# A state recurrence over 96 chunks: 95 steps in sequence, or an up-sweep and a down-sweep with steps of 1, 2, 4, 8 and 16 chunks; and twelve weight splits moved from GpSimd to VectorE

## The chip, the cores and the metric

The kernel runs on one core of a Trainium2 chip. It is one program, one launch. The metric is the device time of that launch in microseconds. Of the core's engines five appear below: TensorE (PE in the profile; PEld is its weight load), VectorE (DVE), ScalarE (ACT), GpSimd (POOL) and SyncE (SP), which here only starts transfers.

## The reference

The kernel computes one layer over 512 latent tokens (8 rows of a grid 64 wide) with 256 context tokens, model width 1024, all in float32. Cut to what matters here:

```python
hx = modulate(x, ...); hc = modulate(ctx, ...)            # RMSNorm, scale, shift
u_x, k_x, v_x, q_x, ga_x, gb_x = split(hx @ w_in)         # 512, 512, 512, 512, 1024, 1024
u_c, k_c, v_c = split(hc @ w_in[:, :1536])
# S5: per direction (forward, backward), 32 groups, 64 complex states each
s_ctx = scan(lam, B u_c)                 # s[t] = lam * s[t-1] + B u[t] over the 256 context tokens
s_lat = scan(lam, B u_x, s0=s_ctx end)   # goes on over the 512 latent tokens
y     = d * u_x + sum over directions of Re(C s_lat)      # only the latent y is wanted
branch_a = glu(gelu(y)) @ w_branch_a
branch_b = neighbourhood_attention(q_x, k_x, v_x, k_c, v_c, bias) @ w_branch_b   # 8 heads of 64
x = x + gate1 * ((sigmoid(ga_x) * branch_a + sigmoid(gb_x) * branch_b) @ w_out)
x = x + gate2 * peer(modulate(x, ...))   # product-key retrieval of 128 experts for each token
```

The recurrence is linear, so any grouping of its steps that multiplies by the right powers of lam gives the same states. Of the context only the state at its end is used.

## The kernel before, in words

**Chunks.** The kernel cuts the 768 tokens into 96 chunks of 8 (`TC = 8`): 32 of the context (`CC`), then 64 latent ones (`CL`). TensorE computes for each chunk what its own tokens add to the state at its end, into the tile `E` of shape [128, 2, 32, 97]: 128 partitions (64 states forward, 64 backward, the latter stored in reversed order), real and imaginary part, 32 groups, and 97 chunk positions, position 0 being zero. The chunk is the innermost index: neighbouring chunks are 4 bytes apart, neighbouring groups 388. Over the chunks the recurrence is E[p] += lam^8 * E[p-1]. The tile `L8` ([128, 2, 2, 32]) holds lam^8 for the complex product: `L8[:, 0]` its real part twice, `L8[:, 1]` its imaginary part with both signs.

**The scan.** `scan_step` (L588 to L595) is one step of it: four VectorE instructions TENSOR_TENSOR on 128x64 elements (two products, their sum, the addition into E[p]). L597 calls it for p = 1 to 95. The states at the 64 latent chunks' starts are copied into the tile `S`, forward ones by GpSimd (L618), backward ones in reversed order by ScalarE (L619), two copies of 64x2048 each. `S` is read by `y_part` (L646), which computes eight parts of y on TensorE. The states' pool (with `E`) is closed behind the q projections (L630), and what `y_load` (L636) fetches for `y_part` takes its place.

**Projections and their weights.** `project` (L447 is the last of the lines of its matmuls) multiplies a 1024x128 block of weights with the activations in three passes: the weights are split into a high part `whi` (a cast on ScalarE, L174) and the rest `wlo` (a subtraction, L175, 128x1024), and TensorE does whi*high, whi*low, wlo*high. `w_ahead` has the loads and the splits of the next blocks issued ahead; `whi` and `wlo` have two buffers each. Blocks 0 to 3 are u, 4 to 7 k, 8 to 11 v, 12 to 15 q; then come the blocks of the merge, the first of them for gate b. `PJE = lambda m: m>3` (L57) names the engine of the subtraction that `project(m)` has done ahead: GpSimd from k on (of two engines `(dve, gp)[PJE(m)]`), VectorE before.

**Attention and what lies beside it.** From L736 on 32 items (4 row pairs by 8 heads) go through three stages: `att_a` scores on TensorE (L685, L686), adds a bias (VectorE, L687), takes a maximum (L689) and an exponential (ScalarE, L691); `att_b` transposes the probabilities (L698) and copies them (L700); `att_c` multiplies by v (L716). Beside them TensorE does gate b's projections, the eight `y_part`s, and then glu, both branches, gates and merge, in an order that a string gives (`MERGE`). At 356 us, while the merge goes on, the second modulation begins: GpSimd multiplies 32 blocks of its weights (`wm`, L791) as they arrive. The PEER part takes the rest, from about 545 us on.

**Order.** The instructions of one engine run in the order of its queue. That order isn't the program's: the layer that records the kernel interleaves independent work by an estimate of its own, which the listings of the next section but one show. Rows from L1048 and L1049 used below are the last folds of one-hot products in PEER: bf16, rows of 16 elements (32 bytes); L1048 at 128x256 reads two neighbouring elements of each row, L1049 one.

Of the kernel before, what the change touches and what calls it, by code (L numbers as in the profile page):

```python
# [10 lines left out]
F32 = mybir.dt.float32  # L11
# [6 lines left out]
ALU = mybir.AluOpType  # L18
# [10 lines left out]
G = 32  # L29
HG = 16  # L30
TC = 8
CL = SEQ // TC
CC = CTXL // TC
NCK = CL + CC
# [19 lines left out]
WQE = lambda p, i: p or i%2  # L54
CHE = lambda t, n: 0
GE = lambda c: c%4==3
PJE = lambda m: m>3  # L57
LDO = "spxxxxccwwwwwwww1wwww1wwww1r"
CEARLY = 0
FC0 = 6  # L60
# [26 lines left out]
def tile_hybrid(ctx, tc, A, out, dbg=None):  # L87
    nc = tc.nc
    sy, act, dve, gp, pe = nc.sync, nc.scalar, nc.vector, nc.gpsimd, nc.tensor

    def open_pool(**kw):
        cm = tc.tile_pool(reuse_waits="tile", **kw)
        return cm, cm.__enter__()

    def close_pool(*cms):
        for cm in cms:
            cm.__exit__(None, None, None)
# [13 lines left out]
    def bank(tag="mm", bufs=None):  # L111
        bufs = bufs or nb[tag]
        return (psA if tag in ("kk", "yy") else ps).tile([128, 512], F32, tag=tag, name=tag, bufs=bufs)
# [11 lines left out]
    L8 = const.tile([128, 2, 2, G], F32, name="L8")  # L125
# [67 lines left out]
    def w_next(want, eng=gp):  # L193
        i = wpos[2]
        assert wseq[i][:2] == want, (wseq[i], want)
        w_ahead(i + 1, i + 1, eng)
        wpos[2] += 1
        w_ahead(i + 3, i + 2, eng)
        return wsp.pop(i)
# [138 lines left out]
    n = 1  # L338
# [114 lines left out]
    def project(m, ctx_too, eng=None):  # L453
        eng = eng or (dve, gp)[PJE(m)]
        w = w_next(("win", m), eng)
        a = bank()
        mm3(a, w, hxh, hxl, KD)
        if not ctx_too:
            return a, None
        c = bank("mc", 1)  # L460
        mm3(c[:, :CTXL], w, hch, hcl, KD)
        return a, c[:, :CTXL]
# [23 lines left out]
    ecm, ep = open_pool(name="ep", bufs=1, side="right")  # L486
    E = ep.tile([128, 2, G, NCK + 1], F32, name="E")
# [88 lines left out]
    for o in SEQ1:  # L576
        m = nxt[o]
# [7 lines left out]

    kcm, kp_ = open_pool(name="kp", bufs=1)

    def scan_step(p_):  # L588
        ta = ep.tile([128, 2, G], F32, name="ta", tag="ta", bufs=2)
        tb_ = ep.tile([128, 2, G], F32, name="tb_", tag="tb_", bufs=2)  # L590
        pr = E[:, :, :, p_ - 1]
        dve.tensor_tensor(ta, pr, L8[:, 0], op=ALU.mult)  # L592
        dve.tensor_tensor(tb_, pr[:, ::-1], L8[:, 1], op=ALU.mult)
        dve.tensor_tensor(ta, ta, tb_, op=ALU.add)  # L594
        dve.tensor_tensor(E[:, :, :, p_], E[:, :, :, p_], ta, op=ALU.add)  # L595

    for p_ in range(1, NCK):  # L597
        scan_step(p_)

    for m in range(4):  # L600
        k_proj(m)
# [4 lines left out]
    for m in range(4):  # L606
# [4 lines left out]
        for j0, n in ((0, 4), (4, 3)):  # L611
            p = bank("tp")
# [10 lines left out]
    for m in range(4):  # L623
        a, _ = project(12 + m, False)
        av = a.rearrange("p (r j c) -> p r j c", r=8, c=16)
        for e in range(2):
            s, z = slice(64 * e, 64 * e + 64), slice(64 * (1 - e), 64 * (1 - e) + 64)
            gp.memset(qT[2 * m + e][z], 0.0)
            act.activation(qT[2 * m + e][s].rearrange("p (j r c) -> p r j c", r=8, c=16), av[s], AF.Copy, scale=0.125)
    close_pool(ecm)  # L630

    ycm, yp = open_pool(name="yp", bufs=1, side="right")
    Y = yp.tile([128, TC, SSMW // 2], F32, name="Y")
# [132 lines left out]
    for i in range(4):  # L766
        p = bank("tp")
        uL = uLs[i]
        yr = slice(64 * (i // 2), 64 * (i // 2) + 64)
        for n_ in range(TC):  # L770
            pe.transpose(p[:, n_ * CL:(n_ + 1) * CL], Y[yr, n_, i % 2 * 128:i % 2 * 128 + 128], ident[yr, yr])
        dve.scalar_tensor_tensor(uL, uL, dsk[:, i:i + 1], p.rearrange("p (n c) -> p n c", c=CL),
                                 op0=ALU.mult, op1=ALU.add)
# [70 lines left out]
    for o in MERGE:  # L844
        m = cnt[o]
# [106 lines left out]
    for half in range(2):  # L952
        p = bank("tp")
# [426 lines left out]
```

## Time and profile before

| | |
|---|---|
| median of three runs | 1874.2 us (1873.22 to 1884.75) |
| the profiled execution | 1876.31 us, span 1874.5 us |
| mean TensorE clock in it | 0.963 of full speed |
| busy: PE, DVE, ACT, POOL | 1727.8, 1499.0, 808.0, 659.0 us |
| scan on DVE | 95 steps, from 134.0 to 284.9 us |
| k, v and q projections on PE | 140.5 to 226 us |

How to read it: the profile tells for every instruction when it started, how long it took and, where its engine had been idle, which instruction released it. The span is the time from the first to the last instruction. An engine's idle time costs only where the end of the program waits for it, and the page's chain of waits lists the work of which that holds. The clock is a share of TensorE's full speed: 0.5 is 1.2 GHz, 1.0 is 2.4 GHz. Shapes are partitions x elements.

### The profile page before, as it was taken

What the parts mean: (1) busy time and instruction counts of PE and PEld (TensorE: products, weight loads), DVE (VectorE), ACT (ScalarE), POOL (GpSimd) and SP (SyncE); (2) the same over time, 40 slices, a digit from 0 to 9 for tenths busy, and PEclk for the clock granted to TensorE, in tenths of its full rate; (3) what the DMA queues carried; (4) which work ended last, traced back from release to release, by engine and by line L of the source; (5) the groups of instructions that cost most, each with busy time, mean ns of one, the idle gap of its engine ahead of it and who ended that gap; (6) DMA issues with size and microseconds to landing.
All of it is one profiled execution on the core that took longest, in us unless ns stands there. A gap on an engine that the chain in (4) does not pass through costs nothing.

```text
span 1874.5 us, 27846 instructions
## 1 busy us (share of the span) xinstructions
PE 1727.8 (92%) x9941; PEld 1505.1 (80%) x9941; DVE 1499.0 (80%) x3111; ACT 808.0 (43%) x1276; POOL 659.0 (35%) x500
## 2 busy tenths in 40 slices
PE   4989879989999989997479999999999999999997
PEld 1778657767779989986369899999999999998885
DVE  7899995587669998999879788788888888884445
ACT  5362245455555435666433333333333333333333
POOL 3553201166523730010233445444445544440002
PEclk8999989999999999998589999999999999999998
DMA  7342114576744435757599899999999999994432
GB/s 278 114 135 83 62 54 112 175 262 210 254 147 148 143 110 159 216 172 212 146 383 361 293 331 329 341 353 350 321 344 357 319 338 347 327 346 144 127 113 79
DMA packets 186331, 426.18 MB, mean 227 GB/s; under 512 B 25552, under 2 KB 91216, under 8 KB 186192
## 3 DMA queue, kind: packets, MB, share of 16 engines
q1 hardware_dynamic: 84816, 231.44, 36.5%
q0 software_dynamic: 36864, 134.23, 20.0%
q10 hardware_dynamic: 64512, 58.73, 9.7%
q8 instruction: 78, 1.28, 0.3%
q14 instruction: 61, 0.50, 0.1%
HBM read 388.72 MB, written 35.62 MB: 226 GB/s over the span
## 4 chain that ended last, share of the span: by engine, by line
PE 71%; DVE 18%; DMA 4%; issue 3%; ACT 2%; POOL 2%; ACTq 0%; SPq 0%; DVEq 0%; POOLq 0%
PE acc L1251 9%; PE acc L1252 9%; PE acc L1253 9%; PE yy L447 5%; PE yy L445 5%; PE yy L446 5%; PE kk L447 5%; PE kk L445 5%; PE kk L446 5%; PE mm L447 2%; PE mm L446 2%; PE mm L445 2%; DVE E L595 2%; DVE ta L592 1%; DVE ta L594 1%
## 5 line engine op out<-in xcount | busy, mean ns | idle before, releaser
L174 ACT CAST whi<-wraw 128x1024 fp32r<-128x1024 f32 (+1 forms) x212 | 213.6, 1008 | 165.5 <-issue 49.9
L175 DVE TENSOR_TENSOR wlo<-wraw,whi 128x1024 fp32r<-128x1024 f32 (+1 forms) x174 | 225.1, 1294 | 56.9 <-ACT whi L174 49.4
L1134 POOL DMA_INDIRECT gu<-in_pu_dram,idx x128 | 173.8, 1357 | 262.5 <-DVE gj L1141 217.4
L1134 POOL DMA_INDIRECT gu<-in_pv_dram,idx x128 | 167.0, 1305 | 161.1 <-DVE gacc L1152 135.4
L1233 DVE TENSOR_TENSOR wlo<-wraw,whi 128x1024 fp32r<-128x1024 f32 x128 | 157.5, 1231 | 41.4 <-ACT whi L1232 37.6
L1152 DVE SCALAR_TENSOR_TENSOR gacc<-gu,av,gacc 128x1024 f32<-128x1024 f32 x127 | 162.6, 1281 | 25.5 <-DMA gu<-in_pv_dram,idx 25.0
L447 PE MATMUL yy<-hth,wlo 128*128 128x384 f32 x512 | 174.9, 342 | 3.6 <-DVE wlo L175 3.6
L1141 DVE SCALAR_TENSOR_TENSOR gj<-gu,hrow 128x1024 bf16<-128x1024 f32 x128 | 156.0, 1219 | 23.4 <-DMA gu<-in_pu_dram,idx 22.9
L445 PE MATMUL kk<-hth,whi 128*128 128x384 f32 x512 | 173.3, 338 | 1.0 <-ACT ring L932 1.0
L445 PE MATMUL yy<-hth,whi 128*128 128x384 f32 x512 | 173.9, 340 | 0.0
L446 PE MATMUL yy<-htl,whi 128*128 128x384 f32 x512 | 173.9, 340 | 0.0
L447 PE MATMUL kk<-hth,wlo 128*128 128x384 f32 x512 | 172.9, 338 | 0.6 <-DVE wlo L175 0.5
L446 PE MATMUL kk<-htl,whi 128*128 128x384 f32 x512 | 172.7, 337 | 0.0
L1232 ACT CAST whi<-wraw 128x1024 fp32r<-128x1024 f32 x128 | 134.0, 1047 | 81.5 <-PE yy L446 30.8
L175 POOL TENSOR_TENSOR wlo<-wraw,whi 128x1024 fp32r<-128x1024 f32 x38 | 96.1, 2532 | 91.5 <-ACT whi L174 87.8
L1120 ACT ACTIVATE gs<-mm 128x512 f32<-128x512 f32 x96 | 95.1, 1088 | 61.4 <-PE mm L1118 59.6
L791 POOL TENSOR_TENSOR wm<-wm,cb 128x1024 f32<-128x1024 f32 x32 | 82.4, 2575 | 87.8 <-DMA wm<-in_wmodT_dram 43.2
L447 PE MATMUL mm<-hxh,wlo 128*128 128x512 f32 x256 | 102.2, 399 | 6.6 <-DVE wlo L175 6.6
L445 PE MATMUL mm<-hxh,whi 128*128 128x512 f32 x256 | 100.0, 395 | 2.6 <-ACT whi L174 2.6
L447 PEld LDWEIGHTS yy<-hth,wlo 128*128 128x128 f32 x512 | 97.2, 190 | 5.7 <-DVE wlo L175 4.2
L446 PE MATMUL mm<-hxl,whi 128*128 128x512 f32 x256 | 100.8, 394 | 0.0
L445 PEld LDWEIGHTS kk<-hth,whi 128*128 128x128 f32 x512 | 96.4, 188 | 3.6 <-ACT ring L932 1.6
(2079 smaller groups left out, 4636.7 us busy)
## 6 DMA issues: line engine op xcount, KB each, us to landing
wraw<-in_puT_dram SPq DMA_DIRECT2D x128, 512.0 KB
wraw<-in_pv_dram SPq DMA_DIRECT2D x128, 512.0 KB
Gt_d<-gs ACTq DMA_DIRECT2D x24, 1024.0 KB
gch<-Gt_d ACTq DMA_DIRECT2D x32, 768.0 KB
wraw<-in_win_dram SPq DMA_DIRECT2D x32, 512.0 KB
wm<-in_wmodT_dram SPq DMA_DIRECT2D x32, 512.0 KB
wraw<-in_wq_dram SPq DMA_DIRECT2D x32, 512.0 KB
wm<-in_wm_dram SPq DMA_DIRECT2D x16, 512.0 KB
```

Of the source, the lines that this page charges most:

```text
L174: act.copy(hi[:, :kn], raw[:, :kn])
L175: i = eng.tensor_sub(lo[:, :kn], raw[:, :kn], hi[:, :kn].bitcast(F32))
L445: pe.matmul(o, hi[:, k], xh, start=(k == 0), stop=False)
L446: pe.matmul(o, hi[:, k], xl, start=False, stop=False)
L447: pe.matmul(o, lo[:, k], xh, start=False, stop=(k == kn - 1))
L1134: gp.indirect_dma_start(out=u, out_offset=None, in_=A[tab], in_offset=bass.IndirectOffsetOnAxis(ap=ix[:, s:s + 1], axis=0))
L1141: dve.scalar_tensor_tensor(jk, u, 1.0, hrow, op0=ALU.mult, op1=ALU.mult, accum_out=av[:, s:s + 1])
L1152: dve.scalar_tensor_tensor(gacc, u, av[:, s:s + 1], gacc, op0=ALU.mult, op1=ALU.add)
L1233: dve.tensor_sub(lo, w, hi.bitcast(F32))
L1251: pe.matmul(acc[t][half], wh_[:, ts], hi[:, cs], start=(j == 0), stop=False)
L1252: pe.matmul(acc[t][half], wh_[:, ts], lo[:, cs], start=False, stop=False)
L1253: return pe.matmul(acc[t][half], wl_[:, ts], hi[:, cs], start=False, stop=(j == 127))
```

## The change

The scan's 95 steps are replaced by 16 calls of `carry(l, first, step, n)`. One call does n chunk positions at once: the positions first, first + step, ... get lam^(8*2^l) times the value 2^l positions before. It is four VectorE instructions on 128x64xn elements. The powers lam^16 to lam^128 are computed by 24 small instructions (four times six, up to 128x32 or 128x64 elements).

- Context, up-sweep only: l = 0 to 4 with n = 16, 8, 4, 2, 1. It leaves the right value in position 32, the end of the context.
- Handover to the first latent chunk: l = 0, n = 1.
- Latent chunks, up-sweep l = 0 to 4 with n = 31, 15, 7, 3, 1, then down-sweep l = 4 to 0 with n = 1, 3, 7, 15, 31.

The innermost index of these instructions is the position, in steps of 2 << l elements: 8 bytes at l = 0, 16 to 128 bytes at l = 1 to 4 (n = 1 has no neighbours but the groups, 388 bytes apart). At l = 0 there are 16 + 1 + 31 + 31 = 79 positions, at l = 1 to 4 there are 15 + 26 + 26 = 67. Both products read `E`, both additions read and write it. A new pool holds the powers and the products' tiles, until the states' pool is closed.

The second part is `PJE = lambda m: 0`: the twelve subtractions (L175) that were on GpSimd in the k, v and q projections, for blocks 5 to 15 and the first block of the merge, are on VectorE.

```diff
-PJE = lambda m: m>3
+PJE = lambda m: 0
...
-    def scan_step(p_):
-        ta = ep.tile([128, 2, G], F32, name="ta", tag="ta", bufs=2)
-        tb_ = ep.tile([128, 2, G], F32, name="tb_", tag="tb_", bufs=2)
-        pr = E[:, :, :, p_ - 1]
-        dve.tensor_tensor(ta, pr, L8[:, 0], op=ALU.mult)
-        dve.tensor_tensor(tb_, pr[:, ::-1], L8[:, 1], op=ALU.mult)
-        dve.tensor_tensor(ta, ta, tb_, op=ALU.add)
-        dve.tensor_tensor(E[:, :, :, p_], E[:, :, :, p_], ta, op=ALU.add)
-
-    for p_ in range(1, NCK):
-        scan_step(p_)
+    sccm, scp = open_pool(name="scp", bufs=1, side="right")
+    lam = [L8]
+    for l in range(4):
+        a_, b_ = lam[-1], scp.tile([128, 2, 2, G], F32, name=f"lam{l}")
...
+        lam.append(b_)
+
+    def carry(l, first, step, n):
+
+        ta = scp.tile([128, 2, G, 31], F32, name="ta", tag="ta", bufs=1)[:, :, :, 0:n]
+        tb_ = scp.tile([128, 2, G, 31], F32, name="tb_", tag="tb_", bufs=1)[:, :, :, 0:n]
+        d = 1 << l
+        to = E[:, :, :, first:first + (n - 1) * step + 1:step]
+        fr = E[:, :, :, first - d:first - d + (n - 1) * step + 1:step]
+
+        def bc(j):
+            return lam[l][:, j].rearrange("p r (g o) -> p r g o", o=1).to_broadcast([128, 2, G, n])
+
+        dve.tensor_tensor(ta, fr, bc(0), op=ALU.mult)
+        dve.tensor_tensor(tb_, fr[:, ::-1], bc(1), op=ALU.mult)
+        dve.tensor_tensor(to, to, ta, op=ALU.add)
+        dve.tensor_tensor(to, to, tb_, op=ALU.add)
+
+    for l in range(5):
+        carry(l, 2 << l, 2 << l, CC >> (l + 1))
+    carry(0, CC + 1, 1, 1)
+    for l in range(5):
+        carry(l, CC + (2 << l), 2 << l, (CL >> (l + 1)) - 1)
+    for l in (4, 3, 2, 1, 0):
+        carry(l, CC + (3 << l), 2 << l, (CL >> (l + 1)) - 1)
...
-    close_pool(ecm)
+    close_pool(sccm, ecm)
```

Lines behind the scan are 25 later in the changed kernel (L687 is L712 there, L619 is L644). How the two kernels' instructions stand in the queues:

VectorE before, at the place where attention begins. L592 to L595 are a scan step (tiles `ta`, `tb_`, `E`), L687 is the attention's first bias addition and L689 its maximum:

```order
L592 TENSOR_TENSOR ta<-E,L_78 128x64
L593 TENSOR_TENSOR tb__2042<-E,L_78 128x64
L687 TENSOR_TENSOR mm<-mm,bs 128x256
L594 TENSOR_TENSOR ta<-ta,tb__2042 128x64
L689 TENSOR_REDUCE nm<-mm 128x1
L595 TENSOR_TENSOR E<-E,ta 128x64
L592 TENSOR_TENSOR ta<-E,L_78 128x64
```

Seventy-seven of the 95 steps stand ahead of that addition in the queue, and the rest of them are interleaved with the attention's own instructions.

VectorE now, at the same place. L612 to L615 are the four instructions of a carry (here the last two of the down-sweep, l = 1 and l = 0; the elements are 64 times the positions, and 1984 is 64x31), L175 the splits, L712 the attention's first addition:

```order
L612 TENSOR_TENSOR ta<-E,lam_1582 128x64x15
L613 TENSOR_TENSOR tb__1699<-E,lam_1582 128x64x15
L614 TENSOR_TENSOR E<-E,ta 128x64x15
L615 TENSOR_TENSOR E<-E,tb__1699 128x64x15
L612 TENSOR_TENSOR ta<-E,L_78 128x1984
L613 TENSOR_TENSOR tb__1705<-E,L_78 128x1984
L175 TENSOR_TENSOR wlo<-wraw,whi 128x1024
L614 TENSOR_TENSOR E<-E,ta 128x64x31
L175 TENSOR_TENSOR wlo<-wraw,whi 128x1024
L615 TENSOR_TENSOR E<-E,tb__1705 128x64x31
L175 TENSOR_TENSOR wlo<-wraw,whi 128x1024 x2
L712 TENSOR_TENSOR mm<-mm,bs 128x256
```

The whole scan and all the splits of the projections stand ahead of the attention's first addition now.

ScalarE before, around its copies of the states (`S<-E`). L672 starts the load of a bias, L691 is the exponential, L700 copies transposed probabilities:

```order
L700 COPY PT<-tp 128x256
L691 ACTIVATE P,ssum<-mm,nm 128x512
L672 DMA bs<-in_bias_dram 128x256
L700 COPY PT<-tp 128x256
L691 ACTIVATE P,ssum<-mm,nm 128x512
L619 COPY S<-E 64x2048 x2
L672 DMA bs<-in_bias_dram 128x256 x2
L700 COPY PT<-tp 128x256
L691 ACTIVATE P,ssum<-mm,nm 128x512
```

ScalarE now. L174 is the cast of a weight split, L640 a copy of v, L654 the two copies out of a q projection, L697 the start of a bias load:

```order
L640 COPY V_1962<-tp 128x4x128
L174 CAST whi<-wraw 128x1024
L640 COPY V_1963<-tp 128x3x128
L654 ACTIVATE q_2264<-mm 64x8x4x16 x2
L644 COPY S<-E 64x2048 x2
L697 DMA bs<-in_bias_dram 128x256 x2
L654 ACTIVATE q_2264<-mm 64x8x4x16 x2
L174 CAST whi<-wraw 128x1024
L697 DMA bs<-in_bias_dram 128x256 x2
L174 CAST whi<-wraw 128x1024
L654 ACTIVATE q_2265<-mm 64x8x4x16 x2
```

The copies of the states stood among the attention's items; they stand now inside the q projections, ahead of q block 1's copies and of the casts for q block 3 and for the merge's first block.

## Rows read from the trace of the kernel before

**Rows 1.** The page's part 1: busy time (share of the span) and instructions of each engine.

```profile
PE 1727.8 (92%) x9941; PEld 1505.1 (80%) x9941; DVE 1499.0 (80%) x3111; ACT 808.0 (43%) x1276; POOL 659.0 (35%) x500
```

**Rows 2.** The page's part 4, the chain of waits: shares of the span by engine.

```profile
PE 71%; DVE 18%; DMA 4%; issue 3%; ACT 2%; POOL 2%; ACTq 0%; SPq 0%; DVEq 0%; POOLq 0%
```

**Rows 3.** Windows: start:end, length, then busy time of each engine, TensorE clock, DMA share, GB/s.

```profile
140.50:226.00 85.50, 85.46 (x471) 73.73 (x468) 79.42 (x234) 26.58 (x60) 31.59 (x35) 1.00 0.25 79
226.00:236.00 10.00, 0.00 (x0) 0.00 (x0) 8.99 (x39) 0.00 (x0) 0.00 (x0) 0.71 0.00 0
236.00:246.00 10.00, 0.08 (x1) 0.08 (x2) 9.14 (x38) 2.20 (x4) 0.00 (x0) 0.50 0.04 13
246.00:251.26 5.26, 4.90 (x14) 3.46 (x14) 5.08 (x19) 2.60 (x6) 0.00 (x0) 0.56 0.22 74
251.26:262.00 10.74, 10.74 (x77) 7.97 (x78) 10.08 (x34) 6.27 (x17) 0.21 (x1) 1.00 0.26 76
...
356.35:545.00 188.65, 172.57 (x724) 135.22 (x725) 138.56 (x133) 104.03 (x171) 104.89 (x47) 0.98 0.67 225
```

**Rows 4.** Timeline of PE: start, duration, line, instruction [idle before it, and its releaser].

```profile
245.92 1.12 PE L698 MATMUL tp<-ident,P 128*128 128x128 f32 x4 [19.96 <-ACT P L691]
```

**Rows 5.** Timeline of DVE: three scan steps, and the attention's first add.

```profile
214.48 2.27 DVE L594 TENSOR_TENSOR ta<-ta,tb__1904 128x64 f32<-128x64 f32 x1
217.10 0.27 DVE L592 TENSOR_TENSOR ta<-E,L 128x64 f32<-128x64 f32 x1
...
217.59 0.23 DVE L594 TENSOR_TENSOR ta<-ta,tb__1910 128x64 f32<-128x64 f32 x1
...
218.16 0.27 DVE L592 TENSOR_TENSOR ta<-E,L 128x64 f32<-128x64 f32 x1
...
242.51 0.42 DVE L687 TENSOR_TENSOR mm<-mm,bs 128x256 f32<-128x256 f32 x1
```

**Rows 6.** Timeline of POOL: one split of projection weights.

```profile
214.28 2.39 POOL L175 TENSOR_TENSOR wlo<-wraw,whi 128x1024 fp32r<-128x1024 f32 x1 [3.31 <-ACT whi L174]
```

**Rows 7.** One line's instructions: duration min/median/max in ns, first and last start.

```profile
L595 DVE TENSOR_TENSOR E<-E,ta x95: 223/278/2512, 134.0 to 284.9; 128x64 f32<-128x64 f32 x95
```

**Rows 8.** Timeline of DVE: other TENSOR_TENSORs, contiguous.

```profile
15.70 0.21 DVE L330 TENSOR_TENSOR tg<-pw 128x64 f32<-128x64 f32 x1
...
17.93 0.28 DVE L331 TENSOR_TENSOR pw<-pw 128x128 f32<-128x128 f32 x1
...
108.57 0.41 DVE L334 TENSOR_TENSOR Gc<-PG,crt 128x256 f32<-128x256 f32 x1
...
678.76 1.19 DVE L175 TENSOR_TENSOR wlo<-wraw,whi 128x1024 fp32r<-128x1024 f32 x1
```

**Rows 9.** Groups of DVE instructions by shape: busy us, mean ns of one, idle before.

```profile
L1048 DVE TENSOR_TENSOR oh<-oh 128x256 bf16<-128x256 bf16 x8 | 3.2, 428 | 0.0
...
L1049 DVE TENSOR_TENSOR v<-oh 128x128 f32<-128x128 bf16 x2 | 0.7, 375 | 0.0
```

**Rows 10.** Timeline of ACT: casts of projection weights, each at a projection's end.

```profile
157.63 1.05 ACT L174 CAST whi<-wraw 128x1024 fp32r<-128x1024 f32 x1 [2.32 <-PE mc L446]
...
201.44 1.05 ACT L174 CAST whi<-wraw 128x1024 fp32r<-128x1024 f32 x1 [1.90 <-PE mc L446]
...
207.45 1.05 ACT L174 CAST whi<-wraw 128x1024 fp32r<-128x1024 f32 x1 [4.20 <-issue]
...
218.59 1.05 ACT L174 CAST whi<-wraw 128x1024 fp32r<-128x1024 f32 x1 [3.17 <-issue]
...
219.67 1.20 ACT L629 ACTIVATE q<-mm 64x512 f32<-64x512 f32 x2
```

**Rows 11.** One line's instructions: ACT's copies of the states.

```profile
L619 ACT COPY S<-E x2: 1901/1904/1908, 287.1 to 288.9; 64x2048 f32<-64x2048 f32 x2
```

**Rows 12.** Waits: engine (SPq is SP's queue), line, releaser: total us, times, longest.

```profile
POOL wm L791 <- DMA wm<-in_wmodT_dram: 43.2, 24, 3.5
...
SPq L643 <- DMA bs<-in_bias_dram: 13.8, 5, 4.1
```

More of the change, by code (lines that the diff above doesn't have):

```diff
@@ L586, in tile_hybrid @@
     kcm, kp_ = open_pool(name="kp", bufs=1)
-    def scan_step(p_):
-        ta = ep.tile([128, 2, G], F32, name="ta", tag="ta", bufs=2)
-        tb_ = ep.tile([128, 2, G], F32, name="tb_", tag="tb_", bufs=2)
-        pr = E[:, :, :, p_ - 1]
-        dve.tensor_tensor(ta, pr, L8[:, 0], op=ALU.mult)
-        dve.tensor_tensor(tb_, pr[:, ::-1], L8[:, 1], op=ALU.mult)
-        dve.tensor_tensor(ta, ta, tb_, op=ALU.add)
-        dve.tensor_tensor(E[:, :, :, p_], E[:, :, :, p_], ta, op=ALU.add)
-    for p_ in range(1, NCK):
-        scan_step(p_)
+    sccm, scp = open_pool(name="scp", bufs=1, side="right")
+    lam = [L8]
+    for l in range(4):
+        a_, b_ = lam[-1], scp.tile([128, 2, 2, G], F32, name=f"lam{l}")
+        ta = scp.tile([128, G], F32, tag="lt", name="lt", bufs=2)
+        dve.tensor_mul(ta, a_[:, 1, 1], a_[:, 1, 1])
+        dve.tensor_mul(b_[:, 0, 0], a_[:, 0, 0], a_[:, 0, 0])
+        dve.tensor_sub(b_[:, 0, 0], b_[:, 0, 0], ta)
+        dve.scalar_tensor_tensor(b_[:, 1, 1], a_[:, 0, 0], 2.0, a_[:, 1, 1], op0=ALU.mult, op1=ALU.mult)
+        dve.tensor_copy(b_[:, 0, 1], b_[:, 0, 0])
+        dve.tensor_scalar(b_[:, 1, 0], b_[:, 1, 1], -1.0, None, op0=ALU.mult)
+        lam.append(b_)
[18 more added lines that the diff above has]
+        carry(l, CC + (3 << l), 2 << l, (CL >> (l + 1)) - 1)
     for m in range(4):
```

## The prediction

> **What bounds the kernel now.** I read the page first: TensorE is busy 92% of the span [rows 1], and 71% of the chain of waits is its own, 18% VectorE's [rows 2]. The reader is to see there that a change to VectorE's work is worth something only where TensorE stands still. So the next view is the windows. TensorE is without a gap through the k, v and q projections (85.46 of 85.50 us), then does nothing in two windows of 10 us while VectorE is 90% busy, works at half clock (0.50 to 0.56) until 251.26, and is full again from there [rows 3]. The timelines name the cause: TensorE's pause of 19.96 us ends at 245.92 with an exponential of the attention [rows 4], and the addition ahead of that exponential ran on VectorE only at 242.51 [rows 5]. It stood in VectorE's queue behind 77 steps of the scan, which lasts from 134.0 to 284.9 [rows 7].
>
> One step takes 1.06 us (217.10 to 218.16). While GpSimd does a split (2.39 us, [rows 6]), the step's instruction takes 2.27 us in place of 0.23 [rows 5]; that happens 11 times between 139 and 222 us. So the scan costs 95 x 1.06 = 101 us and about 11 x 2.05 = 23 us of stalls. The price of the present order is what lies between 225.96, where the q projections end (245.92 less 19.96), and 251.26: 25.3 us, in which TensorE did 4.90 us of half-clock work, 2.45 us at full clock.
>
> **The change: what the new scan costs.** VectorE's price in two kinds of access has to be found.
>
> - Contiguous: 64, 128 and 256 elements took 0.21, 0.28 and 0.41 us [rows 8]. The slope is (0.41 - 0.21)/192 = 1.04 ns an element. Started back to back they lie about 0.07 us further apart than their elements; one that needs the result of the one just before takes some 0.12 us more (the steps' own pitch of 1.06 us for four shows it).
> - One element, then a jump: `ta<-E` at 64 elements, each 388 bytes from the next, took 0.27 us where 0.21 is the contiguous price [rows 5, 8]: +0.9 ns an element. L1049 at 128 elements 32 bytes apart took 0.375 for 0.28 [rows 9, 8]: +0.75. I take the middle, 1.04 + 0.83 = 1.87 ns an element.
> - Two neighbours, then a jump: L1048 at 256 took 0.428 for 0.41 [rows 9, 8], so nothing.
>
> The carries at l = 0 have 78 positions with neighbours 8 bytes apart, 78 x 64 x 4 = 19,968 elements; those at l of 1 and more (16 to 128 bytes apart) and the handover have 68, 17,408 elements. No row shows steps of 8 bytes. I take the contiguous price, since two elements lie in 16 bytes there as two lie in 32 in L1048. Sum: 19,968 x 1.04 = 20.8, 17,408 x 1.87 = 32.6, 64 x 0.07 = 4.5, 32 x 0.12 = 3.8: **61 us**. If all went at 1.04 it would be 47, if all at 1.87 it would be 78. The 24 small instructions add about 3 us.
>
> The Trainium skill, SBUF — State Buffer (Specifications), speaks against the upper levels: lines of 16 bytes, full bandwidth only with at least two accesses to a line. The rows agree for single elements, 0.375 for 0.28 us. By the two accesses every level from l = 1 on pays and level 0 goes free, the 61 us that the rows give by themselves. The page also says that each crossing to a new line pays; level 0 crosses at every second element, and if that counts, its sum is about 69 us by 0.42 ns an element (an estimate from half of the rows' 0.83).
>
> **Its place in time.** The twelve splits on VectorE cost 1.19 us each [rows 8], 14.3 us in all; the stalls of 23 us go, since GpSimd has no split left there. A split can't run before its cast on ScalarE, and a cast marks the end of a projection. VectorE is paced by these up to the split of block 8, done at 157.63 + 1.05 + 1.19 = 159.9 [rows 10]. About 7.5 of the 61 us come before it, 4.3 us (the two additions at 64x31) after q block 1's split; 49 us of scan and five splits (6 us) lie between. So q block 1's weights are ready at 215, where TensorE has been ready for them since 207.45 [rows 10]: 7.5 us late. This is a new stall, TensorE waiting for VectorE inside the projections. The scan ends at 215 + 2.1 + 1.2 + 2.1 = 220.5.
>
> ScalarE's two copies of the states (1.9 us each, [rows 11]) wait for that end, and behind them now stand q block 1's copies (1.20, [rows 10]) and the cast for q block 3 (1.05), then its split (1.19). These weights are ready at 220.5 + 3.8 + 1.2 + 1.05 + 1.2 = 227.8. TensorE is ready after q blocks 1 and 2 of 5.6 us each (half of 207.45 to 218.59, [rows 10]), at 226.2: 1.6 us late. Projections end at 227.8 + 5.6 = 233.4 and, with 2 us for a lowered clock after the stall of 7.5 us, at **235.5**. The bounds of that last term are 0 and 2.5, what the half-clock stretch behind the present pause lost [rows 3]. By the same steps it is 226.8 with 47 us of scan (nothing late but q block 3, by 0.5) and 249.8 with 78 us (q block 1 late by 18).
>
> From there to dense work: from the first addition to the first transposes it was 245.92 - 242.51 = 3.4 us [rows 4, 5], and 2.45 us are the first pieces at full clock. Dense at 241.3 where it was 251.26: **10 us gained**.
>
> **The rest, part by part.**
> - GpSimd: loses twelve splits, on which nobody waited except the scan. In the stretch before 159.9 VectorE has one split more and GpSimd one fewer: 0, within 2 us either way.
> - The scan's last 18 steps and the copies of the states no longer lie among the attention's items. TensorE is full there already (10.74 of 10.74 us from 251.26, [rows 3]), so this cover was complete and its going gives nothing.
> - `y_load` and `y_part` come earlier in the attention, since `S` is ready earlier. SP's loads for them wait for bias loads (13.8 us in 5 waits, [rows 12]). A late one would hold TensorE in its order: I take -2 us, bounds 0 and -10, most of those waits.
> - From there on TensorE's order is the old one, with the y parts about 32 matmuls earlier, so the pools that the second modulation takes come free earlier against TensorE's work. In its stretch TensorE is idle for 188.65 - 172.57 = 16.1 us [rows 3], and GpSimd waits 43.2 us for the arriving weights [rows 12], so most of it hangs on transfers. I take 3, bounds 0 and 16.
>
> Sum: 10 + 3 - 2 = 11 us. Against the profiled execution (1876.3 us; span 1874.5, 1.8 around it) that is **1865 us**. That execution lies 2.1 us above the median of the runs, 1874.2; against the median the gain would read as 9.
>
> **The rivals.**
> 1. *All of E is read at the contiguous price.* For it: instructions of some 1,000 elements may hide what 64 show. Against: L1049. The q projections end at 226.8, dense work starts at 230 to 232, 20 us gained: 1855. Chance 0.2.
> 2. *Level 0 pays as well.* For it: each access of two neighbours in L1048 is 4 bytes in all, while here every element is its own step. Then the q projections end at 249.8, dense work begins at about 256, 5 us later than now: 1880, slower. It decides at about 1.6 ns an element at level 0, where TensorE reaches the dense stretch at 251; with writes dearer still, 2.1 ns on all, the projections end at 258 and it is 1889. The stall has then only moved from behind the projections into them. Chance 0.13. The Trainium skill's penalty for each crossing (SBUF — State Buffer, Specifications) points this way by half; no row of the trace shows it at 8 bytes.
> 3. *The y loads hold the attention.* GpSimd and ScalarE copy `S` at the same moment as the first bias loads are started, and the loads of `y_load` queue behind both. For it: the 13.8 us of waits. Against: they are no longer than 4.1 us each, and eight matmul groups lie between two parts. 7 to 10 us lost instead of 2: 1870 to 1873. Chance 0.12.
> 4. *The merge gives its idle time back.* The second modulation begins 7 us earlier against TensorE's work and takes most of the 16 us: 1852. For it: the weights' transfers are bound by free buffers. Against: the same transfers, at 225 GB/s, keep their pace whenever they start. Chance 0.13.
>
> **How the numbers follow.** My forecast, 1859 to 1872 with the likeliest at 1865, has 0.42. A measurement of this kernel can tell about 1% from no change, 18.7 us: below 1855.5 or above 1892.9. Faster: half of rival 1 and nearly all of rival 4, 0.22. Slower: only the far end of rival 2 and what I have not seen, 0.06. The rest, 0.72, is the same. The range, 1849 to 1881, holds the forecast, rivals 1 and 3, the near ends of 2 and 4, and leaves out what both unknown prices at their ends together would give.
>
> **What will show it.** The additions at 64x31 (l = 0) at 2.1 us and those at 64x15 (l = 1) at 1.9 us: the two prices; 3.8 and 1.0 are rivals 2 and 1. The first wait of TensorE on a split in the q projections, about 7.5 us, and a second of some 2 us behind the cast for q block 3. The last addition into `E` at 220 to 221; projections ended at 235 and TensorE full from 241. No VectorE instruction of 2.3 us between 139 and 222. The stretch of the second modulation with some 13 us idle on TensorE. I would be wrong if the splits came in VectorE's queue ahead of time without delay, or if the stall in the projections passed 17 us.

## The result and the profile after

The changed kernel took 1858.1 us in the median (1855.74 to 1860.64, four runs) where the kernel before took 1874.1 us: a ratio of 0.9912, 95% interval 0.9891 to 0.9932. That is 16 us or 0.9% less: inside the range, 7 us below the predicted 1865, and just short of the 1% that I had set for "faster". Timed again beside another kernel it gave 1857.6 us, ratio 0.9919 (0.9903 to 0.9936). The profiled execution took 1860.64 us, span 1858.8.

The page's part 1 and the shares of its chain of waits, which answer to [rows 1, 2]:

```profile
PE 1728.2 (93%) x9941; PEld 1506.3 (81%) x9941; DVE 1455.7 (78%) x2831; ACT 807.3 (43%) x1276; POOL 627.4 (34%) x488
...
PE 74%; DVE 11%; DMA 4%; issue 4%; POOL 3%; ACT 3%; SPq 0%; ACTq 0%; POOLq 0%; DVEq 0%
```

VectorE lost 43 us of work, and its share of the chain fell from 18% to 11%. The windows that answer to [rows 3], the third cut where the attention's transposes now start (235.20):

```profile
140.50:226.00 85.50, 78.57 (x428) 67.84 (x427) 72.16 (x97) 28.11 (x61) 9.36 (x25) 0.94 0.21 63
226.00:235.20 9.20, 9.20 (x43) 7.60 (x41) 3.68 (x5) 5.41 (x9) 0.00 (x0) 1.00 0.43 128
235.20:246.00 10.80, 10.80 (x72) 7.92 (x71) 9.30 (x20) 7.08 (x19) 0.00 (x0) 1.00 0.71 192
246.00:262.00 16.00, 15.85 (x170) 12.81 (x170) 8.04 (x17) 5.79 (x17) 0.61 (x1) 1.00 0.63 173
```

TensorE's two empty windows behind 226 are gone. In their place 6.93 us are missing in the first one (78.57 of 85.50), inside the projections. Its timeline shows them as one wait, and then the projections' last piece running straight into the attention:

```profile
207.54 0.40 PE L446 MATMUL mm<-hxl,whi 128*128 128x512 f32 x1
214.86 0.80 PE L447 MATMUL mm<-hxh,wlo 128*128 128x512 f32 x1 [6.93 <-DVE wlo L175]
215.45 0.63 PE L445 MATMUL mm<-hxh,whi 128*128 128x512 f32 x1
...
220.50 0.39 PE L445 MATMUL mm<-hxh,whi 128*128 128x512 f32 x1
...
234.77 0.59 PE L711 MATMUL mm<-kTC,q 128*128 128x256 f32 x2
235.20 0.60 PE L723 MATMUL tp<-ident,P 128*128 128x128 f32 x4
```

The matmuls of 128x512 follow each other at 0.43 us from 214.86 to 220.50 and at 0.23 us behind that. A window of 215 to 220 shows the granted clock, 0.50 or 1.2 GHz, with TensorE busy without a gap:

```profile
215.00:220.00 5.00, 5.00 (x12) 3.98 (x13) 5.00 (x3) 0.00 (x0) 0.00 (x0) 0.50 0.53 150
```

Thirteen matmuls at that clock cost 5.64 us where they would be 2.96 at 0.228 us each: 2.7 us. VectorE over the same stretch:

```profile
213.59 1.22 DVE L175 TENSOR_TENSOR wlo<-wraw,whi 128x1024 fp32r<-128x1024 f32 x1
214.72 2.22 DVE L614 TENSOR_TENSOR E<-E,ta 128x1984 f32<-128x1984 f32 x1
216.86 1.22 DVE L175 TENSOR_TENSOR wlo<-wraw,whi 128x1024 fp32r<-128x1024 f32 x1
218.00 2.22 DVE L615 TENSOR_TENSOR E<-E,tb__1705 128x1984 f32<-128x1984 f32 x1
226.30 1.23 DVE L175 TENSOR_TENSOR wlo<-wraw,whi 128x1024 fp32r<-128x1024 f32 x1 [6.09 <-ACT whi L174]
229.08 1.22 DVE L175 TENSOR_TENSOR wlo<-wraw,whi 128x1024 fp32r<-128x1024 f32 x1 [1.55 <-ACT whi L174]
230.22 0.42 DVE L712 TENSOR_TENSOR mm<-mm,bs 128x256 f32<-128x256 f32 x1
```

The split at 213.59 is the one that TensorE waits for, and the scan ends at 220.2. The attention's first addition runs at 230.22, 12.3 us earlier than before [rows 5]. On ScalarE the copies of the states stand behind the scan's end, and q block 1's copies and block 3's cast behind them, as the order said:

```profile
220.25 1.92 ACT L644 COPY S<-E 64x2048 f32<-64x2048 f32 x1 [10.67 <-DVE E L615]
222.07 1.91 ACT L644 COPY S<-E 64x2048 f32<-64x2048 f32 x1
224.00 1.20 ACT L654 ACTIVATE q<-mm 64x512 f32<-64x512 f32 x2
225.22 1.05 ACT L174 CAST whi<-wraw 128x1024 fp32r<-128x1024 f32 x1
```

Stage by stage, of all the kernels that were run (starts of instructions in us, each from its profiled execution; L698 are the attention's transposes; the second modulation's first load is that of its conditioning vector; "x1" is the last transpose of the merged stream, behind which PEER follows; the last column is the start of the last activation). In the scan-alone kernel and in that with q's splits on GpSimd most of a q block or more still lay behind the first L698, as shown below.

| kernel | scan's last | first L698, last | last y part | 2nd modulation's first load | x1 | end |
|---|---|---|---|---|---|---|
| before | 284.9 | 245.9, 325.1 | 351.7 | 356.4 | 573.6 | 1869.8 |
| changed | 218.0 | 235.2, 318.1 | 297.9 | 332.6 | 555.0 | 1854.1 |
| scan alone | 223.8 | 242.1, 336.4 | 316.1 | 350.9 | 569.0 | 1869.7 |
| splits alone | 281.5 | 222.2, 297.4 | 344.6 | 347.8 | 567.2 | 1865.4 |
| q splits on GpSimd | 220.7 | 234.6, 323.2 | 303.0 | 337.7 | 563.0 | 1865.6 |
| the same, copies late | 221.8 | 228.4, 316.0 | 295.7 | 330.4 | 550.9 | 1853.0 |
| positions side by side | 205.7 | 221.8, 305.5 | 285.2 | 320.0 | 543.2 | 1840.8 |
| y held to item 16 | 215.7 | 233.2, 313.6 | 315.0 | 329.7 | 549.9 | 1850.5 |
| y held to item 24 | 215.7 | 233.2, 310.6 | 330.6 | 339.3 | 556.3 | 1856.4 |
| groups inside, E | 208.9 | 230.2, 312.8 | 292.5 | 327.2 | 549.4 | 1846.7 |
| groups inside, E and S | 214.5 | 230.6, 315.1 | 294.8 | 329.5 | 547.3 | 1845.1 |
| changed, again | 215.5 | 233.0, 316.7 | 296.4 | 331.2 | 553.6 | 1850.9 |

### The profile page after: what moved, and what is told of

Read it like the earlier page. It is cut to its first block, busy times and chain, and to the rows that moved or that the text cites. A ratio compares the mean times of both kernels' runs of the same rounds, so it can differ in the third digit from the quotient of the medians.

```text
span 1858.8 us, 27556 instructions
## 1 busy us (share of the span) xinstructions
PE 1728.2 (93%) x9941; PEld 1506.3 (81%) x9941; DVE 1455.7 (78%) x2831; ACT 807.3 (43%) x1276; POOL 627.4 (34%) x488
## 4 chain that ended last, share of the span: by engine, by line
PE 74%; DVE 11%; DMA 4%; issue 4%; POOL 3%; ACT 3%; SPq 0%; ACTq 0%; POOLq 0%; DVEq 0%
PE acc L1276 9%; PE acc L1277 9%; PE acc L1278 9%; PE kk L447 5%; PE kk L446 5%; PE kk L445 5%; PE yy L447 4%; PE yy L445 4%; PE yy L446 4%; PE mm L447 3%; PE mm L445 3%; PE mm L446 3%; DVE wlo L175 2%; DMA wm<-in_wmodT_dram 1%; DMA wor<-in_wout_dram 1%
## 5 line engine op out<-in xcount | busy, mean ns | idle before, releaser
L175 DVE TENSOR_TENSOR wlo<-wraw,whi 128x1024 fp32r<-128x1024 f32 (+1 forms) x186 | 247.0, 1328 | 71.2 <-ACT whi L174 70.6
L174 ACT CAST whi<-wraw 128x1024 fp32r<-128x1024 f32 (+1 forms) x212 | 213.7, 1009 | 128.7 <-PE kk L446 36.8
L1159 POOL DMA_INDIRECT gu<-in_pu_dram,idx x128 | 164.4, 1284 | 253.0 <-DVE gj L1166 205.5
L447 PEld LDWEIGHTS kk<-hth,wlo 128*128 128x128 f32 x512 | 97.6, 191 | 8.6 <-DVE wlo L175 7.4
L445 PEld LDWEIGHTS yy<-hth,whi 128*128 128x128 f32 x512 | 96.3, 188 | 6.4 <-ACT whi L174 3.0
```

Of the source, the lines that this page charges most:

```text
L174: act.copy(hi[:, :kn], raw[:, :kn])
L175: i = eng.tensor_sub(lo[:, :kn], raw[:, :kn], hi[:, :kn].bitcast(F32))
L445: pe.matmul(o, hi[:, k], xh, start=(k == 0), stop=False)
L447: pe.matmul(o, lo[:, k], xh, start=False, stop=(k == kn - 1))
L1159: gp.indirect_dma_start(out=u, out_offset=None, in_=A[tab], in_offset=bass.IndirectOffsetOnAxis(ap=ix[:, s:s + 1], axis=0))
```

## The experiments

**One half of the change at a time.** The scan alone:

```diff
-PJE = lambda m: 0
+PJE = lambda m: m>3
```

> Only the scan is changed; the splits stay on GpSimd. In the queues the first addition of the attention stands behind the whole scan, as in the changed kernel, and ScalarE's two copies of the states stand ahead of the cast for q block 2 (in the changed kernel ahead of the cast for q block 3). Theory 1 (what decides is who stands behind the scan's end in a queue): the scan ends at 220 to 226 (no splits in the queue, but stalls beside GpSimd's), the copies at 224 to 230, q block 2's weights at 228 to 234 where TensorE is ready for them at 213: a stall of 14 to 20 us, projections end at 241 to 247, time 1864 to 1872. Theory 2 (VectorE's time on splits was the price): q block 1's stall of 7 us goes and nothing takes its place, 1848 to 1853.

Measured: 1881.0 us (1876 to 1888, nine runs), ratio to the kernel before 1.0037 (1.0022 to 1.0053). The new scan by itself makes the kernel slower. Neither theory gave that: theory 1's range, a gain, ends 9 us below. Its wait is there all the same. TensorE's timeline has it in the place and of the size that was expected, and ScalarE's shows what stands ahead of the cast:

```profile
230.90 0.80 PE L445 MATMUL mm<-hxh,whi 128*128 128x512 f32 x1 [17.84 <-ACT whi L174]
```

```profile
226.08 1.90 ACT L644 COPY S<-E 64x2048 f32<-64x2048 f32 x1 [23.06 <-DVE E L615]
227.88 1.89 ACT L644 COPY S<-E 64x2048 f32<-64x2048 f32 x1
229.80 1.04 ACT L174 CAST whi<-wraw 128x1024 fp32r<-128x1024 f32 x1
```

ScalarE stood still for 23 us until the scan's end, two copies ahead of a cast that TensorE needed at 213. What theory 1 had wrong is the end of the projections: 255.1 in place of 241 to 247. TensorE didn't finish them behind the wait:

```profile
240.19 1.22 PE L710 MATMUL mm<-kTC,q 128*128 128x256 f32 x2 [3.46 <-ACT P L716]
...
242.77 0.77 PE L447 MATMUL mm<-hxh,wlo 128*128 128x512 f32 x1
...
256.20 0.43 PE L741 MATMUL kk<-PT,V 128*64 128x128 f32 x2
```

It went on with the attention's scores, waited once more for an exponential, and did most of q blocks 2 and 3 only from 242.77 on. The first product with v starts at 256.20, where it was 250.38 before. The profiled execution is the fastest of the nine (1876.3 us) and ends where that of the kernel before does; the rest of the median's loss isn't in it. The splits alone, on the old kernel:

```diff
-PJE = lambda m: m>3
+PJE = lambda m: 0
```

> Only the splits are moved to VectorE; the scan is the old one of 95 steps. The first addition of the attention now stands behind 67 steps in VectorE's queue where it stood behind 77. Theory 1 (the gain comes from the addition getting its turn earlier, whatever the scan looks like): 242 us less ten steps (11 us) less 23 us of stalls beside GpSimd's splits plus 13 us for eleven splits gives the addition at about 221 to 228, TensorE full from about 232 where it was 251, scan's end near 275, time 1855 to 1862. Theory 2 (the sweeps make the gain): 1870 to 1876.

Measured: 1871.9 us (1866 to 1880, ten runs), ratio 0.9989 (0.9971 to 1.0007), no difference: in theory 2's range and 10 us above theory 1's. The first half of theory 1 holds all the same. The attention's first addition runs at 217.4, and TensorE waits nowhere over a microsecond up to the attention, whose second transposes follow at 225.45:

```profile
225.45 0.66 PE L698 MATMUL tp<-ident,P 128*128 128x128 f32 x4 [0.57 <-ACT P L691]
```

The attention starts more than 20 us earlier than before and ends at 297 instead of 325. But the states are copied only at 281.8, so the loads for y start at 285.6, and the y parts run from 307 to 344.6. Two windows of this kernel, the attention and what follows up to the second modulation's first load:

```profile
226.00:297.40 71.40, 70.56 (x502) 51.70 (x502) 59.24 (x198) 39.20 (x107) 6.22 (x6) 1.00 0.27 74
297.40:347.80 50.40, 36.78 (x318) 29.41 (x316) 10.14 (x17) 13.10 (x25) 0.00 (x0) 0.90 0.54 138
```

TensorE is idle for 13.6 of the 50.4 us there and partly at the lower clock. So neither half gains by itself, and theory 1's step that failed is that an earlier attention is enough: the splits bring the attention forward, but y then comes too late; the scan brings y forward, but its end holds up the casts.

**The two waits in the projections.** Only q blocks 1 to 3 on GpSimd:

```diff
-PJE = lambda m: 0
+PJE = lambda m: m in (12, 13, 14)
```

> The changed kernel with the splits for q blocks 1, 2 and 3 on GpSimd, so that none of them waits behind the scan in VectorE's queue. Theory 1: q block 1's stall (6.9 us) and the half-clock stretch behind it go, but ScalarE's copies of the states, which wait for the scan's end at about 220, still stand ahead of the cast for q block 3; TensorE is ready for that block at 219 and gets it at about 228, so the stall only moves by two blocks: 1856 to 1860, as the changed kernel. Theory 2 (the first stall is all there is): 9 us faster than the changed kernel, 1847 to 1851.

Measured: 1871.5 us (1863 to 1876, nine runs), ratio 0.9967. The wait for q block 1 is gone, and one of 8.65 us stands at q block 3, for the cast behind the copies:

```profile
227.82 0.80 PE L445 MATMUL mm<-hxh,whi 128*128 128x512 f32 x1 [8.65 <-ACT whi L174]
```

So the stall moved as theory 1 said; the time is 11 us above its range. Of the 11.5 us that this profile ends later than the changed one's, 8.0 stand at x1, after an attention that ended 5.1 later; 3.5 come in PEER. The attention took that long because the rest of q block 3 lay in it. Behind the wait TensorE went on with scores, transposes and the first product with v (237.34, where the changed kernel has 237.46), and did 22 of that block's 24 matmuls only then, 5.2 us up to 244.92:

```profile
239.68 0.58 PE L447 MATMUL mm<-hxh,wlo 128*128 128x512 f32 x1
```

Then the same with the copies put behind the projections (`mark[0]` is the last split on GpSimd, `last_q` the last copy out of a q projection; the changed kernel's loop of copies goes):

```diff
-    for r in range(2):
-        gp.tensor_copy(S[0:64, r], E[0:64, r, :, CC:CC + CL])
-        act.copy(S[64:128, r], E[64:128, r, :, CC + CL - 1:CC - 1:-1])
...
+    for r in range(2):
+        with tc.issue_after(mark[0]):
+            gp.tensor_copy(S[0:64, r], E[0:64, r, :, CC:CC + CL])
+        with tc.issue_after(last_q):
+            act.copy(S[64:128, r], E[64:128, r, :, CC + CL - 1:CC - 1:-1])
     close_pool(sccm, ecm)
```

> The splits for q blocks 1 to 3 on GpSimd, and the copies of the states put behind the q projections in ScalarE's and GpSimd's queues. Theory 1 (both queues made TensorE wait, one behind the other): no wait of TensorE over 2 us in the q projections, which end at 226 to 229; attention's transposes at 228 to 232 where the changed kernel has 235.2, and a pause of up to 4 us there for the copies; time 1848 to 1854. Theory 2 (what the projections gain is lost behind them, since the attention waits for the scan's end on VectorE in any case): 1856 to 1860.

Measured: 1855.3 us, ratio 0.9890 (0.9868 to 0.9912), by the ratios 14 us below the last one for the place of four copies, and 1 us above theory 1's range. No wait is left in the projections, but two are behind them:

```profile
228.42 0.66 PE L724 MATMUL tp<-ident,P 128*128 128x128 f32 x4 [3.27 <-ACT P L717]
234.15 0.69 PE L742 MATMUL kk<-PT,V 128*64 128x128 f32 x2 [3.00 <-ACT PT L726]
```

The first waits for the exponential, since the scan's end still stands ahead of the attention's addition, and that end came only at 224.0: beside GpSimd's three splits three VectorE instructions took 3.99, 3.97 and 4.42 us in place of 1.9 and 2.2 (last section). The second wait is for ScalarE, which copies states from 230 to 233.7. Against the changed kernel the difference of 2 to 3 us isn't clear of the spread.

**The price of the steps.** The same carries on positions side by side (this leaves out the recurrence's own positions, so the kernel doesn't compute the layer):

```diff
-        to = E[:, :, :, first:first + (n - 1) * step + 1:step]
-        fr = E[:, :, :, first - d:first - d + (n - 1) * step + 1:step]
+        to = E[:, :, :, first:first + n]
+        fr = E[:, :, :, first - d:first - d + n]
```

> All carries of the changed kernel on positions side by side, in the same number and size, so that no instruction with more than one position jumps between the positions; the values of the recurrence are left wrong by that. Theory 1 (an element alone in its 16 bytes costs 1.9 to 2.0 ns, others 1.1): the instructions at 128x960 fall from 1.90 to 1.10 us, at 128x448 from 1.09 to 0.55, the scan becomes 12 to 14 us shorter, q block 1's wait of 6.9 us goes, attention's transposes at 227 to 231; time 1848 to 1854. Theory 2 (the size of the instruction sets its price, not the step): durations and time unchanged, 1856 to 1860.

Measured: 1848.6 us, ratio 0.9849 (0.9816 to 0.9882). Additions at l = 1 (960 elements) and l = 0 (1984) in this kernel, and at l = 1 in the changed one:

```profile
194.67 1.16 DVE L615 TENSOR_TENSOR E<-E,tb__1699 128x960 f32<-128x960 f32 x1
...
205.68 2.22 DVE L615 TENSOR_TENSOR E<-E,tb__1705 128x1984 f32<-128x1984 f32 x1
```

```profile
207.35 1.92 DVE L615 TENSOR_TENSOR E<-E,tb__1699 128x960 f32<-128x960 f32 x1
```

With a step of 16 bytes 960 elements cost 1.92 us, without one 1.16; a step of 8 bytes costs nothing (2.22 us in both kernels). The scan ends 12 us earlier, the wait for q block 1 is gone, the attention begins at 221.8 and the end comes 13 us earlier; against the changed kernel's second profile it is 10 for the scan and 10 for the end. Theory 1 holds in the durations and the time. For the attention's start its range was 5 us too late.

What it doesn't have is that the step still counts beyond 16 bytes. In the changed kernel 448 elements at l = 2 (32 bytes) take as long as 512 at l = 1 (16 bytes):

```profile
L615 DVE TENSOR_TENSOR E<-E,tb__1663 x1: 1072/1072/1072, 189.6 to 189.6; 128x448 f32<-128x448 f32 x1
L615 DVE TENSOR_TENSOR E<-E,tb__1621 x1: 1090/1090/1090, 159.6 to 159.6; 128x512 f32<-128x512 f32 x1
```

**Which end counts behind the attention.** The y loads held back until the attention's item 16 (then, in a second kernel, item 24):

```diff
+        if b < 2:
+            gp.tensor_copy(gt[:, 0, 0, 0:1], ssums[2][:, 0:1])
...
-    y_load(0)
-    y_load(1)
...
-        if i % 3 == 2 and i // 3 < 8:
-            y_part(i // 3)
+        if i == 14:
+            y_load(0)
+            y_load(1)
+        if i > 16 and i % 2:
+            y_part((i - 17) // 2)
```

> The changed kernel with the loads for y held back until the attention's item 16 (a copy of one element into their tiles) and the y parts placed behind that; the rest is unchanged. In the changed kernel the second modulation's first load went out at 332.6 where it was 356.4, 24 us earlier, while TensorE's dense stretch began only 13 us earlier. Theory 1 (that chain from the states over the y loads to the second modulation gives the further gain of the merge): its first load goes back to 345 to 357 and 4 to 8 us of the gain are lost, 1862 to 1867. Theory 2 (the merge gains for another reason): 1856 to 1860.

Measured: 1856.2 us, ratio 0.9891 (0.9874 to 0.9908). My theory 1 fails: the loads began at 267.5 in place of 236.2, the last y part came at 315.0, and nothing was lost. The second modulation's first load went out at 329.7, no later than in the changed kernel (332.6 and 331.2), since the last y part came only 1.4 us behind the attention's end (313.6). That left the later of the two ends as the theory, and so `ssums[3]` in place of `ssums[2]`, which is item 24, with one y part in each item from there on:

> As the kernel with y held back, but the y loads wait for the attention's item 24 instead of 16. Theory 1 (glu starts when the later of two is done, the attention or the y parts; holding to item 16 used up only slack): loads from about 292 to 330, the last y part at 335 to 345 where the attention ends at 313 to 318, the second modulation's first load at 340 to 350, 10 to 18 us lost: 1866 to 1874. Theory 2 (y is hidden however late): 1853 to 1860.

Measured: 1862.7 us, ratio 0.9933 (0.9915 to 0.9951), 6.5 us more than with item 16. Last y part 330.6, last attention 310.6, first load of the second modulation 339.3, each a few us earlier than I expected. The direction is theory 1's, and the loss is less than the 10 us it had at least; against the changed kernel it is 5 us, with intervals that overlap. The window between the two ends shows why:

```profile
310.60:339.30 28.70, 28.70 (x228) 22.58 (x226) 9.60 (x17) 11.36 (x20) 0.00 (x0) 1.00 0.60 155
```

TensorE is full there with other projections, as it was in the kernel before between its two ends (31.22 of 31.30 us from 325.1); what is late is only the second modulation.

**A layout that keeps the whole computation.** The groups innermost, so that chunks are 128 bytes apart and each step of the sweeps reads runs of 32 neighbours (the tiles and the broadcast follow):

```diff
-    E = ep.tile([128, 2, G, NCK + 1], F32, name="E")
+    E = ep.tile([128, 2, NCK + 1, G], F32, name="E")[:].rearrange("p r c g -> p r g c")
```

> The changed kernel, whole, with the states laid out as [128, 2, 97, 32]: the 32 groups of a chunk are neighbours, the chunks 128 bytes apart, so that every level of the sweeps reads and writes runs of 32 elements. Theory 1 (the step between elements sets VectorE's price): all instructions of the sweeps go at the contiguous price, as with positions side by side; the scan ends at 206 to 209, no wait of TensorE in the q projections, the attention's transposes at 221 to 226; 1846 to 1852. Theory 2 (the price returns elsewhere: ScalarE's 48 copies into E and the copies of the states now jump by 128 bytes, and the q casts wait behind the latter): the copies out of E take 3 us or more in place of 1.9, attention not before 230, 1853 to 1858.

Beside it ran the changed kernel once more:

> The changed kernel as it is, beside the one with the other layout, so that both are timed on one chip. Both theories: 1855 to 1861.

Measured side by side: 1854.8 (ratio 0.9904, 0.9887 to 0.9921) and 1857.6 us. VectorE's part is theory 1's: 1.15 us at 960 elements, no wait for q block 1. But theory 2 holds for the rest. The copies out of E now step by 128 bytes, on ScalarE and on GpSimd:

```profile
L644 ACT COPY S<-E x2: 3901/3964/4027, 211.1 to 215.1; 64x2048 f32<-64x2048 f32 x2
```

```profile
L643 POOL COPY S<-E x2: 3879/3933/3987, 211.2 to 215.1; 64x2048 f32<-64x2048 f32 x2
```

They take twice the 1.9 us of [rows 11], and TensorE waits 3.30 us for the cast behind them. The attention starts at 230.2 and the time is 1854.8, where theory 2 put them. So S got the same layout (the copies then run through the groups innermost on both sides):

```diff
-    S = xs_.tile([128, 2, G, CL], F32, name="S")
+    S = xs_.tile([128, 2, CL, G], F32, name="S")[:].rearrange("p r c g -> p r g c")
```

> The kernel with the 32 groups innermost in E, and now in S too, so that the copies of the states read and write runs of 32 elements; the y parts' matmuls take S with a step of 128 bytes as their weights. Theory 1 (the copies' 3.9 us each, and the wait of 3.3 us for q block 3 behind them, were all that the other layout had to pay there): copies at 1.9 us, no wait for q block 3, the attention's transposes at 224 to 228, time 1847 to 1853. Theory 2 (the price moves once more, to TensorE's loads of the states): the y parts' weight loads grow from some 0.1 us, the y parts take longer, 1853 to 1857.

Measured: 1850.5 us, ratio 0.9861 (0.9839 to 0.9883). It is the fastest kernel here that computes the layer, 7 us below the changed one by the medians and 10 by the ratios, whose intervals don't overlap. The copies are back at 1.9 us, the wait for block 3 is gone:

```profile
L644 ACT COPY S<-E x2: 1894/1898/1903, 216.7 to 218.5; 64x2048 f32<-64x2048 f32 x2
```

The attention starts at 230.6, later than theory 1 expected. The scan was late from its start in this execution (its first carry's last addition began at 157.65, where the kernel with E's layout alone had 153.42); why isn't settled. Theory 2's effect is there too and costs nothing that can be seen: a weight load of S takes 0.196 us in place of 0.137, and lies under a matmul of 0.27.

## Why the prediction was right, point by point

- **What bounds the kernel.** Right. The splits alone show it: with the attention's addition ten steps earlier in VectorE's queue, and no split on GpSimd beside the scan, the pause of 20 us is gone.
- **The scan's price.** Right. The 64 instructions were busy 63.6 us and overlap, so that from start to start they took 60.8 (the terms of the sum make 61.7). 1984 elements at l = 0 took 2.22 us (2.1 by the sum), 960 at l = 1 took 1.92 (1.87). That 8 bytes cost nothing and 16 bytes do is shown by the kernel with positions side by side (2.22 us with and without the step of 8 bytes, 1.92 against 1.16 with 16). One price for all steps from 16 bytes on was too coarse, as the rows at l = 2 show; the sum held, so this cost it little. By the rule of the Trainium skill, SBUF — State Buffer (Specifications), full bandwidth takes at least two accesses to a line of 16 bytes; the trace agrees at 8 and at 16 bytes. The Trainium skill's penalty for each crossing (the same section) didn't show at 8 bytes.
- **The new stall in the projections.** Right: 6.93 us at q block 1 (7.5), on a split in VectorE's queue, the scan's end at 220.2 (220.5), and 2.7 us for the lower clock (2, bounds 0 and 2.5: just over the bound).
- **The second wait, for q block 3.** Its weights were ready at 227.5 (227.8), but TensorE came to that block only at 228.0 (226.2): the 2.7 us of the lower clock, which the sum adds behind that wait, lie ahead of it. So 1.6 us of the sum didn't come. In the scan-alone kernel and in that with q's splits on GpSimd the same queue made waits of 17.8 and 8.7 us: the mechanism is real, and hidden here by what the first stall cost.
- **From the projections to the dense stretch.** One term of 3.4 us too many. I added the attention's first chain (addition, exponential) behind the projections. It ran beside q block 3: the first scores were made at 228.4, and the first transposes follow the projections at 235.20 without a wait. The dense stretch began 12.9 us earlier by the first product with v (250.38 to 237.46) where I had 10.
- **y loads: -2 us.** It didn't come: the longest wait ahead of a y part's weight load is 0.5 us. Holding the loads back by 31 us cost nothing.
- **Merge and second modulation: +3 us.** Mis-sized. From branch a's first projection to the merge's end 3.2 us were gained, over the output projection 3.3 us more, 6.5 in all. TensorE's idle time fell in both, in sum from 13.9 to 9.5 us. Before, and in the changed kernel:

```profile
375.20:496.70 121.50, 111.04 (x469) 88.11 (x468) 91.44 (x64) 67.94 (x113) 77.13 (x32) 0.99 0.72 240
496.70:549.80 53.10, 49.64 (x215) 39.03 (x215) 32.53 (x59) 25.33 (x44) 20.79 (x13) 0.97 0.54 187
```

```profile
361.60:480.00 118.40, 110.64 (x469) 88.06 (x469) 87.80 (x62) 67.03 (x111) 75.18 (x31) 0.99 0.73 245
480.00:529.80 49.80, 48.09 (x214) 37.41 (x213) 29.82 (x59) 24.49 (x41) 17.75 (x12) 1.00 0.56 190
```

The second modulation's first load went out 24 us earlier (332.6 for 356.4). In the trace it waits for the last of the transposes of y ahead of glu (`SPq L810 <- PE tp L796: 6.7, 1, 6.7`), which read y and stand in TensorE's order behind the attention; so it follows the later of attention and y, and before that was y, at 351.7. I had looked for the pools in TensorE's order and moved them 7 us. The two kernels with y held fit this. So do all twelve profiles: where the load goes out less than 23 us ahead of branch a's first projection (before, splits alone, item 24), 121.2 to 122.5 us lie from that projection to the merge's end, in the other nine 117.3 to 120.6. That the load alone makes the difference isn't shown.
- **What I hadn't counted.** PEER, from x1 to the end, took 1296.2 us before and 1299.1 in the changed kernel; over all eleven profiles but the first it is 1297.3 to 1302.6. That this comes of the change isn't shown. The changed kernel's own two profiles differ by 1.8 us, and the kernel with y held to item 24 took 1300.1 though TensorE, VectorE, ScalarE and GpSimd run PEER in the very order of the kernel before, which the changed kernel doesn't. The cause stays open.

The sum, by the trace: 12.9 us gained at the dense stretch, 13.5 at branch a's first projection, 20.0 at the end of the output projection, 18.6 at x1, 15.7 at the end. The forecast had 11. Four of its misses lean one way: the attention's first chain, the wait for q block 3 and the y loads were counted as costs and didn't come, and the merge's gain was put too small. That the time is no further off owes something to luck, since PEER took 2.9 us more in this profile. The profiled execution of the changed kernel had also begun its scan 2.4 us later than the second one did (the last addition at 218.0 against 215.5), within what executions differ by ahead of the scan.

Of the rivals, the first (all of E at the contiguous price) is refuted by the durations, and its time of 1855 was nearly met all the same, by the terms above. The second fell with the price at 8 bytes. The third didn't occur. The fourth happened in part, at 6.5 of 16 us.

## What to carry to other kernels

Two parts of one change can each be worth nothing or less and together be worth 16 us: ask for each which of two chains that meet later it brings forward, and what then ends last. When a long piece of work becomes few large instructions, look at who stands behind its end in every queue, copies of its result on other engines first; here moving four such copies was worth 14 us where the splits were on GpSimd. And price an instruction by the step of its innermost index, not by its elements alone. Before reading how long a stage took, look whether work of the stage ahead of it was pushed into it.

## What the runs showed of the hardware that was not expected

- A VectorE instruction of the scan and GpSimd's split, started beside each other, take turns, and the second to start is the longer one. In the kernel with q's splits on GpSimd and late copies:

```profile
201.38 1.91 DVE L612 TENSOR_TENSOR ta<-E,lam 128x960 f32<-128x960 f32 x1
203.18 3.99 DVE L613 TENSOR_TENSOR tb__1699<-E,lam 128x960 f32<-128x960 f32 x1
```

```profile
201.77 3.72 POOL L175 TENSOR_TENSOR wlo<-wraw,whi 128x1024 fp32r<-128x1024 f32 x1 [3.78 <-PE tp L639]
```

  The split starts 0.4 us behind a VectorE instruction, which takes its usual 1.91 us, and ends 2.2 us behind that one's end (2.39 alone, [rows 6]); the next VectorE instruction (1.9 alone) ends 1.7 us behind the split. The two other splits there read alike. Which engine loses goes by who starts first rather than by size: in the scan-alone kernel seven of the eight splits beside the new scan keep 2.39 to 2.47 us, and only the one that starts 0.5 us behind an instruction of 2.22 us takes 3.99.
- The step between elements costs ScalarE and GpSimd a factor of two (3.9 for 1.9 us at 64x2048 with 128 bytes), VectorE one of 1.65 at 16 bytes (1.92 for 1.16) and 1.7 at 32 (1.07 for 0.62), TensorE's weight load one of 1.4 at 128 bytes (0.196 for 0.137).
- ScalarE pays it for writing too: its copies into E of 64x384 took 0.82 to 0.84 us in the median in the two kernels with the new layout, where they took 0.47.
